# One hybrid encoder kernel, side work moved from a timed queue to a lower scheduling rank, and the hidden rows of layer 1 turned by quarters

## The chip, the core and the metric

The kernel runs on one core of a Trainium2 chip. The metric is the device time of one execution in microseconds (us); the median of three runs of the kernel before is 1550.26 us (1547.73 to 1551.45).

A core has a matrix engine (TensorE, PE in the profile; its weight loads are PEld), a vector engine (VectorE, DVE), a scalar engine (ScalarE, ACT), a general engine (GpSimd, POOL) and SyncE (SP), which here only issues DMA transfers. Each engine works off its own list of instructions in order and waits on semaphores for the others. Matrix products go to PSUM, eight banks of 128 x 512 words.

## The reference

x is 512 tokens by 2048. Two layers, each:

```python
h = rmsnorm(x, pre_norm_g[l])
z = h @ w_in[l]                       # 2048 x 5952: latents, conv inputs, memory query, gate
q_lat, kv_lat, k_pe, gb, gc, xin, q_mem, gate = split_cols(z)
a_out = mla_attention(q, k, v)        # 8 heads; q, k, v from the normalised latents, rotary part
c_out = short_gated_conv(gb, gc, xin, conv_w[l])
mem_n = rmsnorm(mem, mem_norm_g[l])   # 256 memory tokens
m_out = memory_attention(q_mem, mem_n, w_mk[l], w_mv[l])   # 4 heads
y = concatenate([a_out, c_out, m_out]) * silu(gate)        # 512 x 2048
x = x + rmsnorm(y @ w_o[l], post_norm_g[l])
```

All of it is float32.

## The kernel before

**Float32 products.** An operand is kept as a high part (a cast to fp32r, `wh` for weights) and a low part (operand minus high part, `wl`). A product is three matmuls, high*high, low*high, high*low: the helper `mm3`, L228 to L230. One *unit* is a weight piece of 128 x 1024 words: SP loads it into a raw buffer `wr` (L132), ACT makes `wh` (L157), DVE makes `wl` (L158), TensorE uses it in 12 matmuls of 512 columns. There are three buffers each for `wh` and `wl`, so the split of unit k waits until TensorE is through with unit k-3.

**Fewer products.** The two big projections (h @ w_in and y @ w_o) are made block-wise with seven products P1 to P7 in place of eight, as Winograd's form of Strassen's scheme has it. The price is side sums: sums `T` of weight blocks (DVE, L407, tiles of a pool `tf` with three buffers), and sums `S` of blocks of the activations, made in place (L373 to L385) and then split like the weights, high part on ACT (L233), low part on DVE (L234). `A` are the unsummed activation blocks, split in the same way. A *group* is two column blocks of the projection; its products come in *passes* (lists `HEAD`, `STEADY`, `SECOND`, `LATE`), and each result in PSUM is added by DVE to its slab (L445; `gb`, `gc`, `og` are such slabs).

**Layer edges.** Rows of x are normalised to `hs` (factor r from an ACT square sum, L561; product L567 in layer 0, on ACT L564 in layer 1, where the tile is called `og`), turned by TensorE against the identity into PSUM banks `hps` (L578, 16 transposes for a tile of 128 tokens), and taken to `hT` times the gain: on DVE for tiles 0 and 1 (L580), on ACT for tiles 2 and 3 (L584). The gains' columns `cols` come from a small transpose (L267, L269). Between the layers there are 16 *memory steps*: eight of keys (`mk`, four banks, 24 matmuls of 256 columns) and eight of values (`mv`, two banks, 12 of 512), whose weight pieces carry the gain (L162, L163). In them the tail of layer 0 (post-norm, residual: L1126 square, L1131 gain, L1164 sum, L1171 residual `xr`) runs and tiles 0 and 1 are turned, each as a whole; tiles 2 and 3 are turned in passes P1 and P2 of layer 1's projection.

**What sets the order.** PE and SP run in the order of the program's list of steps (`manual_schedule`); SP's loads run ahead of the steps by a count. DVE, ACT and POOL are put in order by a scheduler by each instruction's rank, which is normally the place where the program emits it. Side work does not stand in the list: `defer(cost, fn)` puts it into a queue; each step adds its `room` to a sum `spare` (at most 2.5), and the head of the queue is emitted when `spare` covers its cost; `until` empties the queue as far as a product needs it, `settle` wholly. In the queue stand the sums S1 to S4 (cost 2.4 each), the splits A11 and A22, the tables for the rotary part, the post-norm pieces (`scale`, 0.7) and the residual.

The residual's rows `xr` are loaded by SP (L1141) and the post-norm gain `g` too (L244), in the same list as the weights.

## Time and profile before

| | |
|---|---|
| median of three runs | 1550.26 us |
| the profiled execution | 1552.12 us |
| its span, first to last instruction | 1550.4 us |
| granted TensorE clock, mean | 0.994 |
| PE busy | 1500.4 us, 97% |
| DVE busy | 1289.0 us, 83% |
| ACT busy | 855.8 us, 55% |
| POOL busy | 41.6 us, 3% |
| DMA read and written | 259.59 MB, 14.68 MB |

1.7 us of the profiled execution lie outside its span. A row of the timeline gives start, duration, engine, line and operation, and in brackets how long the engine stood idle before it and on whom it waited; equal rows that follow each other are merged ("x3"), with their durations summed. A row overlaps the next one a little, so the pitch of an engine is read from the starts. "A:B" rows of the stage view give, for a stretch in us, the busy time of PE, PEld, DVE, ACT and POOL with their instruction counts, then the granted clock, the DMA share and GB/s.

### The profile page before, as it was taken

The page shows a single profiled execution, that of the slowest core. Times are in us where ns is not written, and L with a number is a line of the kernel's source. Part 1 is how long each engine was busy: PE and PEld are TensorE (multiplying, and loading weights), DVE is VectorE, ACT ScalarE, POOL GpSimd, SP SyncE. Part 2 cuts the span into 40 slices and gives each one's busy share as a digit, 9 for nine tenths or more (in the row PEclk, how much of TensorE's full clock was granted, in tenths as well). Part 3 has the DMA queues.
Part 4 walks back from the last instruction along what each step waited for, and adds up shares of the span by engine and source line. Part 5 has one row for each costly group of instructions (what it writes and reads, how often), then busy time and mean ns, then how long its engine had stood idle before and what let it go on. Part 6 is the DMA issues. An engine that isn't in the chain of part 4 may idle for free.

```text
span 1550.4 us, 20284 instructions
## 1 busy us (share of the span) xinstructions
PE 1500.4 (97%) x7613; PEld 1280.3 (83%) x7613; DVE 1289.0 (83%) x1646; ACT 855.8 (55%) x1315; POOL 41.6 (3%) x73
## 2 busy tenths in 40 slices
PE   8999999999999999998989999999999999999987
PEld 6778888998898888877778778888988888888866
DVE  5999889787977668899884999989788686689997
ACT  6633443455557768644586633443454587775543
POOL 1000000010000000000120000000010000000001
PEclk9999999999999999999999999999999999999999
DMA  6677656677482111566966677566666511037673
GB/s 254 195 220 236 196 178 180 178 217 237 150 267 83 42 42 57 174 213 211 349 207 227 205 221 229 187 191 177 184 211 207 164 42 42 28 96 224 210 241 140
DMA packets 147446, 275.59 MB, mean 178 GB/s; under 512 B 17340, under 2 KB 40212, under 8 KB 144020
## 3 DMA queue, kind: packets, MB, share of 16 engines
q1 hardware_dynamic: 144336, 257.48, 53.0%
q0 software_dynamic: 2880, 16.78, 2.9%
q8 instruction: 59, 0.97, 0.3%
q14 instruction: 39, 0.32, 0.1%
q10 hardware_dynamic: 132, 0.05, 0.0%
HBM read 259.59 MB, written 14.68 MB: 177 GB/s over the span
## 4 chain that ended last, share of the span: by engine, by line
PE 73%; DVE 16%; DMA 4%; issue 3%; ACT 3%; POOL 1%; SPq 0%; DVEq 0%; POOLq 0%; ACTq 0%
PE P L229 16%; PE P L230 16%; PE P L228 16%; DVE wl L158 5%; DVE T L407 4%; DMA wr<-in_w_o_dram 2%; PE ptp L989 2%; PE tps L747 1%; PE sc L228 1%; PE sc L229 1%; PE sc L230 1%; PE o L228 1%; PE o L229 1%; PE o L230 1%; PE sc L969 1%
## 5 line engine op out<-in xcount | busy, mean ns | idle before, releaser
L157 ACT CAST wh<-T 128x1024 fp32r<-128x1024 f32 (+1 forms) x220 | 226.1, 1029 | 309.8 <-PE P L230 209.1
L230 PE MATMUL P<-wh,S 128*128 128x512 f32 (+1 forms) x896 | 345.8, 386 | 10.6 <-DVE S L234 10.6
L229 PE MATMUL P<-wl,S 128*128 128x512 f32 (+1 forms) x896 | 346.6, 387 | 9.1 <-DVE wl L158 9.1
L228 PE MATMUL P<-wh,S 128*128 128x512 f32 (+1 forms) x896 | 347.5, 388 | 3.4 <-DVE og L445 3.4
L158 DVE TENSOR_TENSOR wl<-T,wh 128x1024 fp32r<-128x1024 f32 (+1 forms) x220 | 261.1, 1190 | 50.2 <-ACT wh L157 49.5
L157 ACT CAST wh<-wr 128x1024 fp32r<-128x1024 f32 (+1 forms) x188 | 194.7, 1042 | 183.9 <-PE P L230 138.1
L158 DVE TENSOR_TENSOR wl<-wr,wh 128x1024 fp32r<-128x1024 f32 (+1 forms) x188 | 223.7, 1195 | 70.4 <-ACT wh L157 69.4
L228 PE MATMUL P<-wh,A 128*128 128x512 f32 (+1 forms) x656 | 254.0, 387 | 2.0 <-ACT A L233 1.8
L229 PE MATMUL P<-wl,A 128*128 128x512 f32 (+1 forms) x656 | 252.5, 385 | 2.8 <-DVE wl L158 2.8
L230 PE MATMUL P<-wh,A 128*128 128x512 f32 (+1 forms) x656 | 252.1, 384 | 0.0
L229 PEld LDWEIGHTS P<-wl,S 128*128 128x128 f32 x896 | 169.0, 189 | 43.7 <-DVE wl L158 14.2
L230 PEld LDWEIGHTS P<-wh,S 128*128 128x128 f32 x896 | 168.8, 188 | 43.3 <-DVE S L234 13.1
L228 PEld LDWEIGHTS P<-wh,S 128*128 128x128 f32 x896 | 169.0, 189 | 34.1 <-ACT wh L157 4.3
L407 DVE TENSOR_TENSOR T<-wr,wr 128x1024 f32<-128x1024 f32 (+1 forms) x112 | 132.4, 1191 | 18.9 <-DMA wr<-in_w_in_dram 14.4
L229 PEld LDWEIGHTS P<-wl,A 128*128 128x128 f32 x656 | 123.6, 188 | 25.7 <-DVE wl L158 3.7
L228 PEld LDWEIGHTS P<-wh,A 128*128 128x128 f32 x656 | 123.5, 188 | 24.8 <-ACT A L233 2.0
L230 PEld LDWEIGHTS P<-wh,A 128*128 128x128 f32 x656 | 123.4, 188 | 22.9 <-DVE A L234 0.8
L407 DVE TENSOR_TENSOR T<-wr,T 128x1024 f32<-128x1024 f32 (+1 forms) x112 | 132.9, 1191 | 3.3 <-DMA wr<-in_w_o_dram 1.7
L975 ACT ACTIVATE P<-sc,nm 128x512 f32<-128x512 f32 (+1 forms) x96 | 60.4, 631 | 36.3 <-DVE nm L972 36.3
L972 DVE TENSOR_REDUCE nm<-sc 128x1 f32<-128x512 f32 (+1 forms) x96 | 56.9, 595 | 10.7 <-PE sc L970 8.6
L978 ACT ACTIVATE P<-P,rec 128x512 f32<-128x512 f32 (+1 forms) x96 | 62.6, 667 | 5.6 <-DVE rec L977 5.6
L234 DVE TENSOR_TENSOR PT<-ptp,PT 128x512 fp32r<-128x512 f32 (+1 forms) x96 | 56.4, 594 | 8.0 <-ACT PT L233 7.7
(257 smaller groups left out, 2263.1 us busy)
## 6 DMA issues: line engine op xcount, KB each, us to landing
wr<-in_w_in_dram SPq DMA_DIRECT2D x240, 512.0 KB, 4.6
wr<-in_w_o_dram SPq DMA_DIRECT2D x112, 512.0 KB, 4.9
wr<-in_w_in_dram SPq DMA_DIRECT2D x56, 416.0 KB, 3.9
wr<-in_w_mk_dram SPq DMA_DIRECT2D x16, 512.0 KB, 4.4
wr<-in_w_mv_dram SPq DMA_DIRECT2D x16, 512.0 KB, 4.1
wr<-in_w_uq_dram SPq DMA_DIRECT2D x24, 256.0 KB, 3.7
x<-in_x_dram SPq DMA_DIRECT2D x4, 1024.0 KB, 7.2
wr<-in_w_ukv_dram SPq DMA_DIRECT2D x8, 512.0 KB, 3.9
```

Source lines behind the costliest of these rows:

```text
L157: nc.scalar.copy(hi[:, :n], src)
L158: nc.vector.tensor_tensor(lo[:, :n], src, hi[:, :n].bitcast(F32), op=ALU.subtract)
L228: nc.tensor.matmul(ps, ah, bh, start=first, stop=False, **kw)
L229: nc.tensor.matmul(ps, ah, bl, start=False, stop=False, **kw)
L230: nc.tensor.matmul(ps, al, bh, start=False, stop=last, **kw)
L234: nc.vector.tensor_tensor(lo, src, hi.bitcast(F32), op=ALU.subtract)
L407: nc.vector.tensor_tensor(t, a, b, op=ALU.subtract)
L747: nc.tensor.transpose(ps[:, t * P:(t + 1) * P], view(t)[:, j * P:(j + 1) * P], G["ident"])
L972: nc.vector.tensor_reduce(nmax, ps, axis=AX.X, op=ALU.max, negate=True)
L975: nc.scalar.activation(pt, ps, AF.Exp, bias=nmax, accum_out=tot)
L978: nc.scalar.activation(pt, pt, AF.Copy, scale=rec)
L989: nc.tensor.transpose(ps[:, k * P:(k + 1) * P], pt[:, k * P:(k + 1) * P], G["ident"])
```

## The change

1. The queue is gone. `later(k, fn)` emits at once, with a rank that is k places later; sums S and split A22 get `SUMS` = 96, post-norm pieces `SOON` = 48, rotary tables `SLOW` = 200. Split A11 and the residual are emitted in place.
2. Raw buffers go from five to six, `tf` buffers from three to two; the square sum of the post-norm writes to a tile of its own (`junk`) and not to a `tf` buffer.
3. The 16 loads of `g2` (eight, 256 KB) and `xr` (eight, 1 MB) go from SP's queue to GpSimd's.
4. The start of layer 0 is written out by hand for DVE, ACT and POOL as well: `cols` right after the first `hs`, halves of tiles 0 and 1 in another order (the first half of tile 1 taken by ACT), and P1 begins after 24 transposes where there were 32.
5. In layer 1 all four tiles are turned among the memory steps, by quarters (four transposes, one bank): one after each of the 16 steps. The sums of the left operand are emitted after quarters 11 and 15.

```diff
-RAW, TF, PIECES, SLABS = 5, 3, 4, 19
+RAW, TF, PIECES, SLABS = 6, 2, 4, 19
+SOON, SUMS, SLOW = 48, 96, 200
...
-    def add(self, fn, units=(), room=0.0, ahead=None):
+    def add(self, fn, units=(), ahead=None):
...
-    def defer(self, cost, fn):
-        self.queue.append((cost, fn))
...
+    def later(self, k, fn):
+
+        at = self.tc.cur_priority
+        self.tc.cur_priority = at + k
+        fn()
+        self.tc.cur_priority = at + 1
...
-            spare = min(spare + room, 2.5)
-            while self.queue and spare >= self.queue[0][0]:
-                cost, put_off = self.queue.pop(0)
-                spare -= cost
-                put_off()
...
         for f in (one, two, four, three):
-            pr.defer(2.4, f)
+            pr.later(SUMS, f)
...
-    def transpose_rows(l, t, src, halves=(0, 1)):
+    def transpose_rows(l, t, src, quarters=range(4), on=None):
...
-            if t < 2:
+            if (on or (nc.vector if t < 2 else nc.scalar)) is nc.vector:
...
-        pr.defer(1.2, lambda: left.split("A22", tt, b[:, 8:, :]))
+        pr.later(SUMS, lambda: left.split("A22", tt, b[:, 8:, :]))
...
-                    row(st["g", g, j], post_norm_g[l, (2 * g + j) * 512:(2 * g + j + 1) * 512])
+                    nc.gpsimd.dma_start(st["g", g, j], post_norm_g[l, (2 * g + j) * 512:(2 * g + j + 1) * 512]
+                                        .partition_broadcast(P))
...
-                    junk = tf_p.tile([P, 1024], F32, tag="tf", name=nm("junk"))
-                    nc.scalar.activation(junk[:, :512], o, AF.Square, accum_out=st["ssq"][t][:, k:k + 1])
+                    nc.scalar.activation(G["junk"], o, AF.Square, accum_out=st["ssq"][t][:, k:k + 1])
...
-                pr.defer(0.7, scale)
+                pr.later(SOON, scale)
...
-                nc.sync.dma_start(st["x"][t], G["src"][t * P:(t + 1) * P, :])
+                nc.gpsimd.dma_start(st["x"][t], G["src"][t * P:(t + 1) * P, :])
...
-            for h in range(2):
-                for t in range(2):
-                    add(lambda t=t, h=h: transpose_rows(0, t, G[f"hs{t}"], (h,)))
-                    add(lambda t=t, h=h: left_half(t, (h,)))
-            add(lambda: first_rows(2))
-            add(lambda: first_rows(3))
+            def turn_half(t, h, on=None):
+                return lambda: transpose_rows(0, t, G[f"hs{t}"], (2 * h, 2 * h + 1), on)
+            add(turn_half(0, 0))
+            add(lambda: first_rows(1, (0,)))
+            add(pr.begin_prep(1))
+            add(lambda: left_half(0, (0,)))
+            add(pr.begin_prep(2))
+            add(turn_half(1, 0, nc.scalar))
+            add(lambda: first_rows(1, (1,)))
+            add(lambda: left_half(1, (0,)))
+            add(pr.begin_prep(3))
+            add(lambda: first_factor(2))
+            add(turn_half(0, 1))
         else:
             ms = mem_steps(l)
-            put(ms[:3])
+            put(ms[:1])
             add(use)
-            for t in range(2):
-                add(lambda t=t: pr.until(lambda: f"hs{t}" in G))
-                add(turn[t])
-                add(lambda t=t: left_half(t))
-                put(ms[3 + 4 * t:7 + 4 * t])
-            put(ms[11:])
+            for n in range(16):
+                t, q = n // 4, n % 4
+                add(lambda t=t, q=q: transpose_rows(l, t, G[f"hs{t}"], (q,)))
+                if t < 2 and q % 2:
+                    add(lambda t=t, q=q: left_half(t, (q // 2,)))
+                if t >= 2 and q == 3:
+                    add(lambda t=t: right_half(t - 2))
+                put(ms[n + 1:n + 2])
...
-                pr.defer(1.2, lambda: left.split("A11", p, a[:, :, :256]))
-                pr.defer(1.2, lambda: left.split("A22", p, b[:, :, 256:]))
+                left.split("A11", p, a[:, :, :256])
+                pr.later(SUMS, lambda: left.split("A22", p, b[:, :, 256:]))
```

How this moves instructions is seen in three places. The rows below are the engines' own lists, in order (line, operation, output<-inputs, shape; line numbers are those of the kernel in question, the numbers behind names only tell tiles apart).

**DVE, output projection of layer 0, first passes of its first group, before.** `wl` are the low parts of units, `T` weight sums, `y` and `S` the sums of the activations and their splits, `og<-og,P` results added to their slab.

```order
L445 TENSOR_TENSOR og_5797<-og_5797,P_704_6084 128x512
L234 TENSOR_TENSOR S_709_6168<-y_3439,S_709_6168 128x1024
L158 TENSOR_TENSOR wl_6176<-T_710_6173,wh_6175 128x1024
L158 TENSOR_TENSOR wl_6200<-T_713_6197,wh_6199 128x1024
L407 TENSOR_TENSOR T_716_6219<-wr_6143,T_713_6197 128x1024
L377 TENSOR_TENSOR y_3439<-y_3439,y_3752 128x4x256
L407 TENSOR_TENSOR T_719_6241<-wr_6171,T_716_6219 128x1024
L158 TENSOR_TENSOR wl_6222<-T_716_6219,wh_6221 128x1024
L407 TENSOR_TENSOR T_720_6263<-wr_6193,wr_6195 128x1024
```

**The same place now.** `wl_6200`, `wl_6224` and `wl_6246` here are the splits that are `wl_6176`, `wl_6200` and `wl_6222` above.

```order
L156 TENSOR_TENSOR wl_6200<-T_715_6197,wh_6199 128x1024
L371 TENSOR_TENSOR y_3447<-y_3447 128x4x256
L156 TENSOR_TENSOR wl_6224<-T_718_6221,wh_6223 128x1024
L227 TENSOR_TENSOR S_706_6092<-y_3447,S_706_6092 128x1024
L227 TENSOR_TENSOR S_707_6096<-y_3447,S_707_6096 128x1024
L435 TENSOR_TENSOR og_5806<-og_5806,P_711_6113 128x512
L435 TENSOR_TENSOR og_5817<-og_5817,P_712_6114 128x512
L227 TENSOR_TENSOR S_708_6100<-y_3805,S_708_6100 128x1024
L397 TENSOR_TENSOR T_721_6243<-wr_6167,T_718_6221 128x1024
L1120 TENSOR_TENSOR og_5806<-og_5806,g_709_6103 128x512
L1120 TENSOR_TENSOR og_5817<-og_5817,g_709_6103 128x512
L156 TENSOR_TENSOR wl_6246<-T_721_6243,wh_6245 128x1024
```

Between the second and the third of these splits there stood three whole-width operations (two weight sums and one sum of the activations); now there stand four (three splits `S` and one weight sum) and four of half width (two results and two post-norm products), and one sum of the activations stands ahead of the second.

**DVE, output projection of layer 0, pass P3/P1 of its second group, before.** `T_744` and `T_749` are the weight sums T3 and T1 of a chunk; `og<-og,g` is the post-norm's product.

```order
L1131 TENSOR_TENSOR og_5786<-og_5786,g_702_6075 128x512
L1131 TENSOR_TENSOR og_5797<-og_5797,g_702_6075 128x512
L445 TENSOR_TENSOR og_5788<-og_5788,P_732_6461 128x512 x2
L445 TENSOR_TENSOR og_5799<-og_5799,P_733_6462 128x512 x2
L1131 TENSOR_TENSOR og_5788<-og_5788,g_702_6075 128x512
L1131 TENSOR_TENSOR og_5788<-og_5788,g_701_6073 128x512
L1131 TENSOR_TENSOR og_5799<-og_5799,g_702_6075 128x512
L1131 TENSOR_TENSOR og_5799<-og_5799,g_701_6073 128x512
L158 TENSOR_TENSOR wl_6661<-wr_6585,wh_6660 128x1024
L158 TENSOR_TENSOR wl_6667<-wr_6615,wh_6666 128x1024
L407 TENSOR_TENSOR T_744_6617<-wr_6585,wr_6639 128x1024
L407 TENSOR_TENSOR T_749_6641<-wr_6639,wr_6615 128x1024
```

**The same place now** (`T_741` and `T_744`).

```order
L156 TENSOR_TENSOR wl_6552<-T_738_6549,wh_6551 128x1024
L397 TENSOR_TENSOR T_741_6626<-wr_6589,wr_6642 128x1024
L397 TENSOR_TENSOR T_744_6644<-wr_6642,wr_6624 128x1024
L156 TENSOR_TENSOR wl_6568<-wr_6509,wh_6567 128x1024
L435 TENSOR_TENSOR og_5806<-og_5808,P_732_6455 128x512
L435 TENSOR_TENSOR og_5817<-og_5819,P_733_6456 128x512
L156 TENSOR_TENSOR wl_6592<-wr_6529,wh_6591 128x1024
L435 TENSOR_TENSOR og_5808<-og_5808,P_735_6477 128x512 x2
L435 TENSOR_TENSOR og_5819<-og_5819,P_736_6478 128x512 x2
L1120 TENSOR_TENSOR og_5806<-og_5806,g_710_6105 128x512
L1120 TENSOR_TENSOR og_5817<-og_5817,g_710_6105 128x512
L156 TENSOR_TENSOR wl_6661<-wr_6589,wh_6660 128x1024
```

The two sums of the second chunk stood behind ten `og` operations and two splits; they now stand ahead of all of these.

**ACT, memory steps of layer 1, before.** `wh<-wr,cols` are the memory steps' weights (the last is step 16), `wh<-wr` without `cols` the first units of the projection, `Km` and `Vm` the results of keys and values.

```order
L162 ACTIVATE wh_7590<-wr_7516,cols 128x512 x2
L162 ACTIVATE wh_7622<-wr_7536,cols 128x512 x2
L157 CAST wh_7642<-wr_7568 128x1024
L233 CAST Km_7670<-mk_7188 128x256
L233 CAST Km_7670<-mk_7189 128x256
L233 CAST Km_7670<-mk_7190 128x256
L157 CAST wh_7681<-wr_7588 128x1024
L233 CAST Km_7670<-mk_7191 128x256
```

**The same place now.** `hT_7668<-hps_7669` takes the first quarter of tile 3 (quarter 12 of the 16, counted from 0), `hps_7698` the second, `hps_7746` the third.

```order
L226 CAST A_812_7617<-hT_7508 128x1024
L160 ACTIVATE wh_7680<-wr_7547,cols 128x512 x2
L155 CAST wh_7709<-wr_7588 128x1024
L226 CAST S_813_7621<-hT_7508 128x1024
L155 CAST wh_7757<-wr_7636 128x1024
L226 CAST S_814_7625<-hT_7508 128x1024
L226 CAST S_815_7629<-hT_7238 128x1024
L226 CAST S_816_7633<-hT_7508 128x1024
L570 ACTIVATE hT_7668<-hps_7669,cols 128x128 x4
L570 ACTIVATE hT_7668<-hps_7698,cols 128x128 x4
L226 CAST Km_7737<-mk_7208 128x256
```

The first two quarters of tile 3 now stand behind two casts of the projection's weights and four splits `S`; before, tiles 2 and 3 were taken further down, among the projection's units.

More of the change, by code (lines that the diff above doesn't have):

```diff
@@ L165, in prep @@
                 outs[c] = (hi[:, :n], lo[:, :n])
+        self.prep = prep
         c = 0
-        spare = 0.0
-        for units, fn, room, ahead in self.steps:
+        for units, fn, ahead in self.steps:
             n = len(units)
@@ L574, in transpose_rows @@
         g = G[f"g1_{l}"].rearrange("p (k o) -> p k o", o=1)
-        for q in [2 * h + i for h in halves for i in range(2)]:
+        for q in quarters:
             ps = bank("hps")
```

125 lines of the change are left out of this document (66 added, 59 removed).

## The prediction

> **What bounds the kernel now.** I first read the page's busy time, then for whom TensorE waits, and then the stages in which it does.
>
> ```profile
> PE 1500.4 (97%) x7613; PEld 1280.3 (83%) x7613; DVE 1289.0 (83%) x1646; ACT 855.8 (55%) x1315; POOL 41.6 (3%) x73
> ...
> PE P L229 <- DVE wl L158: 11.8, 14, 1.7
> PE P L230 <- DVE S L234: 10.6, 6, 2.9
> PE P L228 <- DVE og L445: 3.4, 2, 2.4
> PE hps L578 <- DVE hT L580: 3.2, 2, 2.8
> ```
>
> TensorE is busy for 97% of the span and the change takes no matmul away, so only its waits can be won. The waits' columns are us in total, times, longest. Nearly all are short waits for DVE: 22 of them, 25.8 us, for low parts, side sums and PSUM results. Over the whole program DVE has room (83%); it hasn't in some stages:
>
> ```profile
> 680.00:720.00 40.00, 38.70 (x171) 31.74 (x170) 38.63 (x43) 19.66 (x30) 0.00 (x0) 1.00 0.55 172
> 720.00:760.00 40.00, 35.33 (x154) 28.40 (x153) 32.59 (x31) 18.15 (x24) 1.61 (x3) 1.00 0.89 316
> 810.00:868.00 58.00, 57.95 (x317) 49.88 (x315) 37.51 (x44) 37.34 (x70) 1.14 (x2) 1.00 0.64 202
> 868.00:960.00 92.00, 86.50 (x369) 69.91 (x369) 87.26 (x85) 39.92 (x40) 0.00 (x0) 0.98 0.70 221
> ```
>
> The third number of a row is DVE: 38.63 of 40 us before 720, 87.26 of 92 in layer 1's projection, but 37.51 of 58 just ahead of that. So the order of DVE's work decides: what is moved from 868:960 into 810:868 is free, what is moved into a full stretch is paid in full. A wait costs more than itself where the granted clock falls behind it:
>
> ```profile
> 18.90:22.30 3.40, 3.36 (x7) 2.26 (x8) 3.40 (x6) 1.57 (x2) 0.00 (x0) 0.50 1.01 381
> 733.00:736.40 3.40, 2.80 (x11) 2.12 (x12) 3.40 (x5) 1.77 (x5) 0.00 (x0) 1.00 0.93 293
> 923.40:926.80 3.40, 3.40 (x10) 2.68 (x9) 3.29 (x4) 0.86 (x1) 0.00 (x0) 0.51 0.55 155
> ```
>
> Shortly after the waits at 18.89 and 921.96 (below) the clock was 0.50 for 3.4 us, which does the work of 1.7 us; after the one at 733.03 it stayed 1.00. I charge 1.5 us for such a stretch.
>
> The pitch of the work, from starts:
>
> ```profile
> 711.78 1.31 DVE L1131 TENSOR_TENSOR og<-og,g 128x512 f32<-128x512 f32 x2
> 713.00 2.36 DVE L158 TENSOR_TENSOR wl<-wr,wh 128x1024 fp32r<-128x1024 f32 x2
> 715.27 2.36 DVE L407 TENSOR_TENSOR T<-wr,wr 128x1024 f32<-128x1024 f32 x2
> ...
> 716.90 0.39 PE L228 MATMUL P<-wh,A 128*128 128x512 f32 x1
> 719.62 0.39 PE L228 MATMUL P<-wh,S 128*128 128x512 f32 x1
> ```
>
> A full-width DVE operation takes 1.135 us (713.00 to 715.27 for two), one of half width 0.61, and the 12 matmuls of a unit 2.72 (716.90 to 719.62). A split is one operation, with a weight sum two, 2.27: DVE gains 0.45 us a unit there, and each operation more between two splits costs 1.135 of its lead, which three low-part buffers limit.
>
> **Start (a gain of 4.4 us).**
>
> ```profile
> 12.71 3.49 DVE L158 TENSOR_TENSOR wl<-wr,wh 128x1024 fp32r<-128x1024 f32 x3
> 16.12 0.24 DVE L269 COPY cols<-cps 128x88 f32<-128x88 f32 x1
> ...
> 16.41 0.66 PE L578 MATMUL hps<-ident,hs 128*128 128x128 f32 x4 [1.82 <-DVE cols L269]
> 18.89 0.80 PE L228 MATMUL P<-wh,A 128*128 128x512 f32 x1 [1.81 <-ACT A L233]
> ...
> PE P L230 <- DVE S L234: 3.8, 2, 2.6
> PE P L229 <- DVE wl L158: 2.3, 3, 0.9
> ```
>
> `cols` stands behind three splits, 3.4 us (12.71 to 16.12), and the last transposes wait for it. Now it stands ahead of them, and eight transposes (0.87) are no longer ahead of P1. P1 starts 3.4 to 4.3 us earlier; I take 4.1. The last two rows are the waits of the first 160 us: 3.8 and 2.3 us, to which a half-clock stretch belongs; all of it, 7.6 us, goes, as the sums are now emitted elsewhere. In their place come two bursts: in the new order four operations stand between the splits of the 11th and 12th units (with the split 5.7 us for a unit of 2.72, 3.0 late), and further on two `S`, two results of half width and two sums ahead of a split (6.9 for 2.72, 4.2 late). 4.1 + 7.6 - 7.2 = 4.5; I take 4.4. Bounds: the bursts swallowed by DVE's lead, 8; a half-clock stretch behind each and half of the old waits left, -2.
>
> **Output projection, first passes (a loss of 6.5).** Before, from `wl_6176` to `wl_6222` there are five full-width operations, 5.7 us for two units (5.4). Now, from `wl_6200` to `wl_6246`, there are seven and four of half width: 7 x 1.135 + 4 x 0.61 = 10.4. That is 4.7 more, twice (both layers have it), 9.4. The waits that stood a little later there,
>
> ```profile
> 672.09 0.50 PE L230 MATMUL P<-wh,S 128*128 128x512 f32 x1 [1.17 <-DVE S L234]
> ...
> PE P L230 <- DVE S L234: 1.5, 1, 1.5
> ```
>
> (layer 0; the second row is the same place of layer 1) were for an `S` that is now made earlier, so 1.2 + 1.5 go: -9.4 + 2.7 = -6.7; I take 6.5. Bounds: 0 with DVE three units ahead, as the late split then finds its unit still covered by 8 us of matmuls; 10 if nothing goes.
>
> **Output projection, late passes (a gain of 10).** In layer 0 between 700 and 745, and in layer 1 from 1430 on:
>
> ```profile
> PE P L229 <- DVE wl L158: 3.6, 3, 1.7
> PE P L228 <- DVE og L445: 2.4, 1, 2.4
> ...
> PE P L229 <- DVE wl L158: 4.0, 4, 1.7
> PE P L228 <- DVE og L445: 1.0, 1, 1.0
> ...
> 722.66 1.05 ACT L157 CAST wh<-wr 128x1024 fp32r<-128x1024 f32 x1 [4.50 <-DMA wr<-in_w_o_dram]
> 720.68 2.36 DVE L407 TENSOR_TENSOR T<-wr,wr 128x1024 f32<-128x1024 f32 x2 [0.78 <-DMA wr<-in_w_o_dram]
> ...
> 731.60 8.37 SPq L1141 DMA_DIRECT2D xr<-in_x_dram  x2
> ```
>
> 11.0 us in all. Their root is raw weights that land late: ACT waits 4.50 us and DVE 0.78 for them, because a chunk holds three of five buffers until its sums are made, and these stood behind ten `og` operations. Now they stand ahead of the `og` operations, there is a sixth buffer, and SP's list holds no `xr` whose wait stops the weights behind it (two issues took 8.37 us at 731.60). I take 10 of the 11; bounds 4 (only the DMA waits go, 5.3 us in layer 0, and not all reaches TensorE) and 11.
>
> **Memory steps of layer 1 (a loss of 2.7).**
>
> ```profile
> 792.09 1.25 PE L578 MATMUL hps<-ident,og 128*128 128x128 f32 x8 [2.83 <-DVE hT L580]
> ...
> 845.54 4.25 ACT L584 ACTIVATE hT<-hps,cols 128x128 f32<-128x128 f32 x16
> 849.55 1.17 ACT L157 CAST wh<-wr 128x1024 fp32r<-128x1024 f32 x1
> 850.49 1.18 ACT L233 CAST A<-hT 128x1024 fp32r<-128x1024 f32 x1
> ```
>
> A tile turned whole waits for its banks' evacuation: six of eight banks are keys and values, so 2.83 at 792.09, and 3.2 with the second. By quarters a bank has two steps to come free (2.72 us for one of values, by the pitch above); the 3.2 go. But quarter 14 needs the bank of quarter 12, and ACT evacuates that behind the cast of the projection's second unit, which waits until TensorE is through with step 15, the step just ahead of quarter 14. So TensorE waits for that cast and three `S` splits (0.95 each, 849.55 to 850.49) and a quarter's evacuation (a fourth of 845.54 to 849.55, 1.0): 4.8, with semaphores and DVE's sum for the last `S` 5. Behind it on ACT stand `Km` and the units' casts. A second place: half of a step's weights behind two evacuations and an `A` on DVE (2 x 0.61 + 1.135 = 2.4), of which I take 0.9. 3.2 - 5.0 - 0.9 = -2.7. Bounds: +3.2, and -7 with both in full and ACT late.
>
> **Projection of layer 1 (a gain of 5).** Waits between 865 and 960:
>
> ```profile
> PE P L230 <- DVE S L234: 4.1, 2, 2.9
> PE P L229 <- DVE wl L158: 1.4, 2, 0.9
> 921.96 0.50 PE L230 MATMUL P<-wh,S 128*128 128x512 f32 x1 [2.90 <-DVE S L234]
> ```
>
> 5.5 us and a half-clock stretch, 7.0. All eight sums are now made before this stretch, in the one with 20 us of room. The first units' casts and splits stand behind quarter 14's backlog; I let them take back 2 of it, +5. Bounds 1 and 7.
>
> **The rest.** The heads, with two `tf` buffers: rotated queries of the next tile must wait for the turn of this one, and TensorE makes that turn ahead of the scores that need ACT next; nothing, +-2. The loads on GpSimd's list: what stands behind them there is the reload of the memory operands, whose own wait ends later than SP's for `xr` did (739.97),
>
> ```profile
> 752.59 0.55 POOL L687 DMA_DIRECT2D mH<-mTd  x1 [295.99 <-DVE wl L158]
> ```
>
> (after 296 us without work), so nothing; if the reload waited, the first memory step would be late by as much. Half-clock stretches behind the new waits of 4.2, twice 4.7, and 5.0 us: the trace has two behind three, I charge two of four, -2.9.
>
> By the Trainium skill, "TensorE: Matmul & The Clock Gate", section "Part 1: The HAM clock gate (the 'warmup' mystery)", the clock halves only after an idle window of about 3.4 us; here it halved after 1.81 and 2.90, so the trace does not bear that out as a bound from below. By it all four new waits would cost a stretch each, 3.1 us more than in my sum.
>
> **Sum**: 4.4 - 6.5 + 10 - 2.7 + 5 - 2.9 = +7.3. The profiled execution took 1552.1 us with 1550.4 of span; it becomes 1544.8. The median of the runs lies 1.9 below it, so I forecast **1543.0**, own range 1536 to 1549.
>
> **Rivals.**
> *The lead swallows the new waits.* A sixth raw buffer and earlier sums could leave DVE three units ahead when the bursts come. Then 6.5, 5.0 and 2.9 of the losses don't come: 1543 - 14.4 = 1528.6; with half of it 1536. For it: 20 us of room just ahead of the projection, and no DMA wait that eats the lead any more. Against it: 38.63 of 40 us at the first passes.
> *No change.* The gains of the late passes and of layer 1's projection are only half, 7.5 less, as DVE's total work there is the same and its waits merely move: 1550.5. For it speaks that the change takes no DVE work away.
> *Slower: two sum buffers.* A sum T may not be written until the split two sums back is done, and that one waits for a low-part buffer; DVE has one sum (1.19 with its row, 1.135 by pitch) less lead wherever TensorE waits for it. Place: the passes with a weight sum for every unit, in both projections. Price: 22 waits x 1.135 = 25 us if each is longer by one, 12.5 if half are: 1543 + 12.5 = 1555.5. It decides from 11 of the 22 on. Against it: DVE's own order already puts a sum one ahead at most in most rows.
>
> **Chances.** Forecast 0.45, swallowed 0.25, no change 0.15, slower 0.15. A measurement tells 0.3%, 4.7 us, from no change, so faster is below 1545.6: two thirds of the forecast's range, the whole second case: 0.56. Within: a third of the first, most of the third, some of the last: 0.28. Slower: 0.16. The range reaches half-way into the last case and to the second case's full price: 1529 to 1555.
>
> **What would show it.** P1 starts near 14.8 in the changed profile; waits of 4 to 5 us for `wl` near 655 and 1417; waits for `wl` and `og` below 1 us from 700 to 745; one wait of `hps` for ACT's `hT` of about 5 us near 825 and none of 2.8 for DVE's; DVE below 90% and no wait for `S` in layer 1's projection. Wrong it would be if DVE's order left TensorE the same sum of waits in other places, about 37 us, or if waits for a weight sum grew all over.

## The result, and the profile after

| | before | changed |
|---|---|---|
| median of runs (range, number), us | 1550.86 (1547.73 to 1552.01, 4) | 1569.27 (1565.95 to 1572.20, 4) |
| ratio, 95% interval | | 1.0121 [1.0092, 1.0151] |
| profiled execution, its span, us | 1552.12, 1550.4 | 1566.91, 1565.1 |
| mean granted clock | 0.994 | 0.991 |

The changed kernel is slower by 1.2%. I had forecast 1543.0 us and a range up to 1555. The page of the changed kernel gives the engines' busy times (us, share of the span, instructions):

```profile
PE 1503.3 (96%) x7613; PEld 1281.2 (82%) x7613; DVE 1298.9 (83%) x1642; ACT 858.9 (55%) x1323; POOL 47.7 (3%) x89
```

TensorE's waits in it (us in total, times, longest):

```profile
PE P L222 <- DVE wl L156: 15.4, 18, 2.3
PE P L221 <- ACT wh L155: 10.5, 6, 3.1
PE hps L564 <- ACT hT L570: 7.4, 1, 7.4
PE P L221 <- DVE og L435: 4.2, 2, 2.2
PE mv L222 <- DVE wl L161: 2.4, 1, 2.4
...
PE P L223 <- DVE S L227: 0.8, 1, 0.8
```

The work is the same. The waits for side sums `S` are nearly gone (10.6 us before, 0.8 now). In their place stand waits for the high parts `wh`, one wait of 7.4 us for a quarter of turned rows, and longer waits for `wl`. All of TensorE's waits sum to 51.4 us, where they summed to 39.6 before.

Waits alone miss what a lower clock costs, so I used a second measure that holds both. All kernels here run the same 7613 TensorE instructions. Each kind has a pitch, the median from one start to the next (0.227 us for a matmul of 512 columns, 0.187 for 416, 0.120 for 256, 0.109 for a transpose of 128); the pitches sum to 1476.4 us in every one of them. The **time lost** up to an instruction is its start less the pitches of all that are ahead of it. The table cuts the program at the same TensorE instructions in every kernel and gives the us lost in each stage; the letters stand for runs that are told of further on.

| stage (its time in the kernel before) | before | changed | e3 | e2 | e5 | e8 | e9 | e10 | e11 | b1 | b2 |
|---|---|---|---|---|---|---|---|---|---|---|---|
| start, to 74 | 13.6 | 8.5 | 12.2 | 9.8 | 12.7 | 13.3 | 12.7 | 12.3 | 9.7 | 14.7 | 14.9 |
| layer 0, projection, to 120 | 6.2 | 7.0 | 2.8 | 7.9 | 2.8 | 2.8 | 2.8 | 2.8 | 7.9 | 4.8 | 5.9 |
| the rest of it, to 493 | 3.3 | 9.9 | 2.8 | 11.5 | 3.0 | 2.8 | 3.3 | 2.9 | 11.3 | 11.3 | 3.3 |
| heads, to 627 | 4.2 | 2.3 | 3.5 | 2.3 | 3.6 | 4.7 | 4.7 | 4.7 | 2.2 | 1.5 | 2.6 |
| output projection, first passes, to 721 | 3.5 | 9.5 | 7.6 | 8.8 | 7.7 | 4.2 | 3.8 | 1.2 | 8.7 | 6.7 | 8.1 |
| its late passes, to 787 | 5.6 | 5.6 | 7.4 | 5.3 | 10.8 | 10.9 | 2.3 | 2.3 | 1.6 | 1.9 | 5.2 |
| last pass, first memory steps, to 833 | 5.9 | 5.6 | 8.2 | 5.5 | 4.6 | 4.6 | 3.9 | 5.4 | 3.9 | 6.0 | 5.4 |
| memory steps to the last, to 862 | 0.1 | 9.5 | 9.7 | 0.1 | 0.1 | 0.1 | 0.1 | 0.1 | 9.0 | 0.1 | 0.0 |
| layer 1, projection, to 951 | 8.1 | 2.1 | -0.1 | 3.8 | 0.7 | 0.7 | 0.7 | 0.7 | 2.0 | 8.4 | 8.0 |
| the rest of it and heads, to 1406 | 5.5 | 9.1 | 7.9 | 9.8 | 7.3 | 9.0 | 8.9 | 7.3 | 9.1 | 8.3 | 7.8 |
| output projection, first passes, to 1438 | 1.8 | 6.0 | 6.6 | 6.5 | 6.3 | 1.5 | 0.0 | 0.0 | 6.4 | 3.2 | 0.9 |
| its late passes, to 1538 | 6.4 | 3.8 | 5.6 | 3.6 | 5.6 | 5.6 | 1.9 | 2.9 | 1.5 | 6.2 | 6.4 |
| sum | 64.1 | 78.9 | 74.3 | 74.7 | 65.1 | 60.2 | 45.1 | 42.5 | 73.3 | 73.1 | 68.4 |

From 64.1 to 78.9 is 14.8 us, and the spans differ by 14.7. So the table holds the loss: +6.6 in the steady part of layer 0's projection, +6.0 and +4.2 in the first passes of the two output projections, +9.4 in the last memory steps, +3.6 in the rest of layer 1. Against it stand -6.0 in layer 1's projection, -5.1 at the start, -2.6 in the last late passes and -1.9 in the heads.

How far a cell can be trusted is seen up to layer 0's heads: there the changed kernel, e2 and e11 run the same instructions in the same order, and their cells still differ by up to 1.6 us, the four rows together by 3.8 (27.7 to 31.5). So the smallest of these differences are not clear of chance; b2, which is the kernel before but for its loads, has 2.6 in the heads and 7.8 in the rest of layer 1 (before: 4.2 and 5.5).

The stages of the changed kernel that answer to those shown of before (busy us of PE, PE's weight loads, DVE, ACT, POOL; granted clock, DMA share, GB/s):

```profile
720.00:760.00 40.00, 36.90 (x160) 30.06 (x161) 35.29 (x35) 18.24 (x24) 3.18 (x6) 1.00 0.84 299
826.00:868.00 42.00, 34.57 (x184) 29.71 (x183) 33.47 (x36) 28.81 (x54) 1.14 (x2) 0.92 0.58 182
868.00:960.00 92.00, 90.39 (x398) 74.31 (x397) 78.74 (x77) 37.54 (x38) 0.00 (x0) 1.00 0.70 219
668.20:671.60 3.40, 3.40 (x9) 2.63 (x10) 3.34 (x4) 2.10 (x2) 0.00 (x0) 0.50 0.52 154
847.70:851.10 3.40, 3.40 (x11) 2.83 (x11) 1.50 (x5) 2.82 (x11) 0.58 (x1) 0.50 0.00 0
```

DVE did get room in layer 1's projection: 78.74 of 92 us, where it had 87.26. The memory steps pay for it: TensorE is busy for 34.57 of 42 us at a clock of 0.92. The last two rows lie in half-clock stretches behind the two kinds of new waits. Each of these lasts 6.8 us in all: from 666.9 to 673.7, and from 844.4 to 851.2, of which 3.0 us fall into the wait itself.

### The profile page after: what moved, and what is told of

It reads as the page before. It is cut to its first block, busy times and chain, and to the rows that moved or that the text cites. A ratio compares the mean times of both kernels' runs of the same rounds, so it can differ in the third digit from the quotient of the medians.

```text
span 1565.1 us, 20352 instructions
## 1 busy us (share of the span) xinstructions
PE 1503.3 (96%) x7613; PEld 1281.2 (82%) x7613; DVE 1298.9 (83%) x1642; ACT 858.9 (55%) x1323; POOL 47.7 (3%) x89
## 4 chain that ended last, share of the span: by engine, by line
PE 48%; issue 24%; DVE 17%; ACT 6%; DMA 4%; POOL 1%; DVEq 0%; SPq 0%; POOLq 0%; ACTq 0%
PE P L222 10%; PE P L223 10%; PE P L221 10%; DVE wl L156 4%; DMA wr<-in_w_o_dram 4%; DVE T L397 3%; PE ptp L979 1%; DVE og L435 1%; PE tps L737 1%; DVE S L227 1%; DVE xr L1160 1%; ACT wh L155 1%; ACT P L965 1%; DVE og L1120 1%; PE qps L223 1%
## 5 line engine op out<-in xcount | busy, mean ns | idle before, releaser
L221 PEld LDWEIGHTS P<-wh,S 128*128 128x128 f32 x896 | 169.1, 189 | 45.1 <-ACT wh L155 15.5
L222 PEld LDWEIGHTS P<-wl,A 128*128 128x128 f32 x656 | 123.4, 188 | 33.5 <-DVE wl L156 12.2
L965 ACT ACTIVATE P<-sc,nm 128x512 f32<-128x512 f32 (+1 forms) x96 | 60.2, 627 | 37.6 <-DVE nm L962 37.5
```

Of the source, the lines that this page charges most:

```text
L221: nc.tensor.matmul(ps, ah, bh, start=first, stop=False, **kw)
L222: nc.tensor.matmul(ps, ah, bl, start=False, stop=False, **kw)
L965: nc.scalar.activation(pt, ps, AF.Exp, bias=nmax, accum_out=tot)
```

## The experiments

My theory after the result: four parts lose, each in its own place: the third sum buffer given up for a sixth raw one, the crowded side sums, the right half's sums ahead of the last quarters, and the post-norm's products that come too early. The rival: all of it is one loss, the two sum buffers (or the loads on GpSimd), and the waits elsewhere follow from it. Times of an experiment stand beside runs of the kernel before on the same chip. Where two versions are compared through their medians, this is said; the chips can differ by 2 us in it, as the kernel before had medians from 1549.96 to 1552.02.

### One part at a time

**e3: the buffers back to five raw and three sums.**

```diff
-RAW, TF, PIECES, SLABS = 6, 2, 4, 19
+RAW, TF, PIECES, SLABS = 5, 3, 4, 19
```

> The changed kernel with five raw and three sum buffers, as before the change. Theory B (with two sum buffers DVE has one sum less lead wherever TensorE waits for it): 10 to 15 us faster, 1553 to 1559 us, and waits for splits of weight sums shorter all over. Theory A: within 3 us of the changed kernel; in the late passes of the output projections the waits for raw weights grow by 1 to 4 us a layer.

1561.54 us (1559.79 to 1562.95, 4 runs), 1.0069 [1.0054, 1.0084]; 7.7 us under the changed kernel's median. In the table the gain stands where a sum buffer should matter: 9.9 to 2.8 in the steady part of layer 0's projection and 7.0 to 2.8 just ahead of it. The wait for the quarter stays the same:

```profile
PE hps L564 <- ACT hT L570: 7.4, 1, 7.4
```

**b1: the kernel before with six raw and two sum buffers.** As in the change, the squares' scratch, which before lay in a sum buffer, got a tile of its own, and the identity and the set-up rows went from tiles of their own to shared small ones.

```diff
-RAW, TF, PIECES, SLABS = 5, 3, 4, 19
+RAW, TF, PIECES, SLABS = 6, 2, 4, 19
...
-                    junk = tf_p.tile([P, 1024], F32, tag="tf", name=nm("junk"))
-                    nc.scalar.activation(junk[:, :512], o, AF.Square, accum_out=st["ssq"][t][:, k:k + 1])
+                    nc.scalar.activation(G["junk"], o, AF.Square, accum_out=st["ssq"][t][:, k:k + 1])
```

> The kernel before with the pools of the change alone: six raw and two sum buffers, a tile of its own for the square sum, the constants' tiles made smaller for it. The queue, the loads on SP, the start and the whole-tile turns stay. Theory B (the third sum buffer is DVE's lead over TensorE): 6 to 12 us slower than the kernel before, 1556 to 1562 us, with the new waits for splits in the passes between 100 and 350 us and at the output projections' begin. Theory A (only the clumped order costs): within 3 us of the kernel before.

1561.23 us (4 runs) against 1552.02 (17): 1.0058 [1.0043, 1.0073], 9.2 us. In the other order, with the old queue, the exchange costs about the same. The place shows how. First DVE of the kernel before, then of b1, at the same results of layer 0's projection (start, duration, out<-in):

```profile
125.86 1.22 DVE L407 TENSOR_TENSOR T<-wr,T 128x1024 f32<-128x1024 f32 x1
127.36 1.23 DVE L158 TENSOR_TENSOR wl<-T,wh 128x1024 fp32r<-128x1024 f32 x1 [0.28 <-ACT wh L157]
...
134.44 0.68 DVE L445 TENSOR_TENSOR gc<-gc,P 128x512 f32<-128x512 f32 x1
135.04 1.22 DVE L158 TENSOR_TENSOR wl<-T,wh 128x1024 fp32r<-128x1024 f32 x1
```

```profile
127.02 1.23 DVE L158 TENSOR_TENSOR wl<-T,wh 128x1024 fp32r<-128x1024 f32 x1 [0.28 <-ACT wh L157]
...
134.10 0.68 DVE L445 TENSOR_TENSOR gc<-gc,P 128x512 f32<-128x512 f32 x1
134.69 1.22 DVE L407 TENSOR_TENSOR T<-wr,T 128x1024 f32<-128x1024 f32 x1
135.83 0.69 DVE L631 TENSOR_TENSOR gc<-gc,xi 128x512 f32<-128x512 f32 x1
136.43 1.22 DVE L407 TENSOR_TENSOR T<-wr,wr 128x1024 f32<-128x1024 f32 x1
137.57 2.50 DVE L158 TENSOR_TENSOR wl<-T,wh 128x1024 fp32r<-128x1024 f32 x2
```

With three buffers the sum that the split at 135.04 reads is made at 125.86, ahead of nine operations of half width on the results and of two splits that have sums of their own. With two, a buffer for it comes free only when the split at 127.02 has read the sum there. By then the results are due, the sum stands behind them (134.69), and its split comes at 137.57, 2.5 us later. TensorE waits there:

```profile
137.12 0.49 PE L228 MATMUL P<-wh,A 128*128 128x512 f32 x1 [0.39 <-ACT wh L157]
138.84 0.50 PE L229 MATMUL P<-wl,A 128*128 128x512 f32 x1 [1.22 <-DVE wl L158]
```

b1 also shows what the exchange is good for: in layer 0's late passes it loses 1.9 us instead of 5.6. Both runs move a raw and a sum buffer at once; the rows above tie the loss to the sums at this place. A kernel with six raw and three sum buffers was not run.

**e2: the right half's side sums behind the 16th quarter.**

```diff
-                if t >= 2 and q == 3:
-                    add(lambda t=t: right_half(t - 2))
                 put(ms[n + 1:n + 2])
+            for tt in range(2):
+                add(lambda tt=tt: right_half(tt))
```

> The changed kernel with one edit: the sums of both pairs of layer 1's hidden rows are emitted after the sixteenth quarter, and not after quarters 11 and 15. Theory A: TensorE's wait of 7.4 us for ACT's evacuation of quarter 12 (near 847 us) goes with its half-clock stretch, 9 us; the sums now fall into the projection's first two passes, where they may cost up to 3 us; 1560 to 1563 us. Theory B and C: the wait stays or its time appears elsewhere, no change in sum.

1563.14 us (4 runs), 1.0082 [1.0067, 1.0097]; 6.1 under the changed kernel's median. The stage of the last memory steps goes from 9.5 to 0.1, and 1.7 of it come back in the projection behind it (2.1 to 3.8). In the changed kernel TensorE waits, and ACT's timeline tells for what:

```profile
847.42 1.12 PE L564 MATMUL hps<-identr,og 128*128 128x128 f32 x4 [7.43 <-ACT hT L570]
...
842.07 1.04 ACT L226 CAST S<-hT 128x1024 fp32r<-128x1024 f32 x1 [1.06 <-DVE hT L367]
844.34 1.99 ACT L226 CAST S<-hT 128x1024 fp32r<-128x1024 f32 x2 [1.23 <-DVE hT L371]
846.24 2.16 ACT L570 ACTIVATE hT<-hps,cols 128x128 f32<-128x128 f32 x8
```

The evacuations that free quarter 14's bank start at 846.24, behind the casts of `S`. Two of these waited another 1.06 and 1.23 us for DVE's sums, which are made in place in `hT`.

**e1: the four sums apart.** Ranks of 96, 96, 288 and 480 instead of 96 for all four.

```diff
-        for f in (one, two, four, three):
-            pr.later(SUMS, f)
+        for k, f in ((1, one), (1, two), (3, four), (5, three)):
+            pr.later(k * SUMS, f)
```

> The changed kernel with one edit: the four side sums of a pair no longer share one lower rank (96 places), they are put apart: S1 and S2 at 96, S4 at 288, S3 at 480. Theory A (sums of one rank stand together in DVE's order, and TensorE waits for the split behind them): the stretch in which the output projection's first passes lose 7 us against the kernel before in layer 0 (near 667 us) and 8 us in layer 1 (near 1440 us), half-clock stretches included, shrinks to 2 us or less each, the 5 us lost near 78 us mostly go too; the whole is 10 to 17 us faster than the changed kernel, 1552 to 1559 us. Theory B (two sum buffers) and theory C (loads through GpSimd): no change, 1565 to 1572 us.

1571.96 us (4 runs), 1.0137 [1.0122, 1.0152]: no gain. Layer 0's first passes lose 8.9 instead of 9.5. With two sum buffers, moving the side sums doesn't help there.

**e4: the 16 loads back on SP's list.**

```diff
-                    nc.gpsimd.dma_start(st["g", g, j], post_norm_g[l, (2 * g + j) * 512:(2 * g + j + 1) * 512]
-                                        .partition_broadcast(P))
+                    row(st["g", g, j], post_norm_g[l, (2 * g + j) * 512:(2 * g + j + 1) * 512])
...
-                nc.gpsimd.dma_start(st["x"][t], G["src"][t * P:(t + 1) * P, :])
+                nc.sync.dma_start(st["x"][t], G["src"][t * P:(t + 1) * P, :])
```

> The changed kernel with the 16 loads of residual rows and post-norm gains back on SP's queue. Theory C (loads through GpSimd cost time): several us faster. Theory A: within 2 us of the changed kernel; if SP's wait for a residual slab stops the weights behind it, as in the kernel before, up to 3 us slower in the late passes of the output projections.

1577.33 us (1572.76 to 1585.37, 4 runs), 1.0182 [1.0144, 1.0220]: 8 us above the changed kernel's median. 7.5 us of the profiled execution's loss stand in the last stage (3.8 to 11.3), and there most of it is one wait, for the last weight sum's high part:

```profile
1550.73 0.79 PE L221 MATMUL P<-T4h,A 128*128 128x512 f32 x1 [4.74 <-ACT T4h L155]
```

In that kernel all four casts of `T4h` stand on ACT behind the squares of a result that DVE takes only after four residual operations. Why the scheduler's order comes out so with the loads back on SP stays open.

**b2: the kernel before, with the 16 loads on GpSimd.** The same lines the other way, in the old order.

> The kernel before with one part of the change: the 16 loads of post-norm gains and residual rows on GpSimd's list. If SP's wait for the residual's slabs holds up the weights of the late passes, as the prediction had it, the waits near 733 and 741 us and the same of layer 1 shrink: 2 to 5 us faster. If those weights were issued ahead of it anyway and DVE's work sets these waits: within 2 us of the kernel before.

1556.93 us (10 runs) against 1551.19 (24): 1.0039 [1.0023, 1.0054], 5 to 6 us. The loss is in layer 0's first passes (3.5 to 8.1). DVE's timeline there, in the kernel before:

```profile
637.59 1.29 DVE L234 TENSOR_TENSOR PT<-ptp,PT 128x512 fp32r<-128x512 f32 x2
...
640.19 1.23 DVE L407 TENSOR_TENSOR T<-wr,T 128x1024 f32<-128x1024 f32 x1 [0.17 <-DMA wr<-in_w_o_dram]
```

And in b2, with GpSimd's first gains and TensorE's wait:

```profile
633.80 1.23 DVE L407 TENSOR_TENSOR T<-wr,T 128x1024 f32<-128x1024 f32 x1 [1.54 <-DMA wr<-in_w_o_dram]
638.25 1.22 DVE L407 TENSOR_TENSOR T<-wr,T 128x1024 f32<-128x1024 f32 x1 [1.97 <-DMA wr<-in_w_o_dram]
...
639.99 1.28 DVE L234 TENSOR_TENSOR PT<-ptp,PT 128x512 fp32r<-128x512 f32 x2
...
634.37 1.10 POOL L1105 DMA_DIRECT2D g<-in_post_norm_g_dram  x2 [176.78 <-PE ptp L989]
...
641.33 0.39 PE L229 MATMUL o<-PT,V 128*128 128x256 f32 x1 [3.13 <-DVE PT L234]
```

The weights of these two sums come earlier in b2, where SP has no gains to issue ahead of them: they land at 633.70 and 638.15, in the kernel before at 640.09 and 642.04. But both sums now stand ahead of the last head's `PT` in DVE's list, DVE stops there for weights, and TensorE waits 3.13 us for `PT` (0.24 before). The gains' transfers can't have made the first of DVE's waits: it was over at 633.80, and GpSimd issued its first gain at 634.37. They may have lengthened the second, as its weight took 6.5 us to land beside them, the first 3.8. So by these rows what costs is DVE's order; why it changes with the loads' place stays open, as in e4.

### Parts together

**e5: e3 and e2 together.**

> The changed kernel with five raw and three sum buffers and the side sums of layer 1 behind the sixteenth quarter. If the two causes are separate places, their gains of 8 and 6 us add: 1553 to 1558 us. If they are the same time counted twice (the lead lost at one place is lost at the next anyway): 1559 to 1562 us.

1554.30 us (10 runs), 1.0013 [1.0003, 1.0024]. Through medians 15.0 us under the changed kernel, and the two parts alone gave 7.7 + 6.1 = 13.8: two losses that add up, so not one. The largest losses left against before, by the table, are the two first passes (7.7 and 6.3) and layer 0's late passes (10.8); the changed kernel, with its sixth raw buffer, loses 5.6 in the last.

**e6: e5 with the sums apart (e1's edit).**

> The one before (three sum buffers, sums behind the sixteenth quarter) with the side sums S put apart in rank (96, 96, 288, 480) as well. With two sum buffers putting them apart gained nothing. If that was because DVE then had no weight sums made ahead, it gains now: the 5 us lost near 663 us and the same place of layer 1 shrink to 2 us or less, 6 to 10 us in all, 1544 to 1551 us. If rank is not what makes these waits: within 3 us of the one before.

1558.25 us (7 runs), 1.0040 [1.0028, 1.0051]. The first passes do gain now, 7.7 to 4.3 and 6.3 to 1.5. But the beginning of layer 0's projection (second row of the table, 2.8 in e5) loses 15.6 (3.7 of it are taken from the row ahead, so 9 in all), as the same function makes the hidden rows' sums there. ACT of e6:

```profile
82.78 1.04 ACT L226 CAST S<-hT 128x1024 fp32r<-128x1024 f32 x1 [6.83 <-DVE hT L375]
83.73 1.07 ACT L443 COPY gb<-P 128x512 f32<-128x512 f32 x2
```

A cast of `S` waits 6.83 us for a sum whose rank is now far down DVE's list, and behind it on ACT stands the copy that frees a result's bank. TensorE's `P` at 84.36 waits 11.71 us for it.

**e7: e6 with the residual at a lower rank still.** The last post-norm piece of a tile emits the residual, which so had rank 48 already; now it has 48 more.

```diff
-                        residual(l, st, t)
+                        pr.later(SOON, lambda: residual(l, st, t))
```

> The one before with the residual, which the change emits in place, at the post-norm's lower rank (48 places) as well. If the 2.5 us wait near 781 us, for a split that stands behind two residual operations which wait for GpSimd's factor, is made by the residual's rank: that wait goes, 2 to 3 us faster in layer 0, and nothing in the tail. Otherwise no change.

1557.07 us (5 runs), 1.0034 [1.0021, 1.0047]. The wait near 781 does go: e6 waits 2.35 us for a split at 783.9 and 2.44 for a step's weights at 808.4, e7 at neither place. The late passes go from 9.1 (e6) to 7.5, the stages behind hardly move, and the medians' 1.2 us lie within both ranges, so as times the two are not told apart.

**e8: e5 with the sums apart in the output projections alone.**

```diff
+        far = (1, 1, 1, 1) if left.by_tokens else (1, 1, 3, 5)
+        for k, f in zip(far, (one, two, four, three)):
+            pr.later(k * SUMS, f)
```

> The changed kernel with three sum and five raw buffers, layer 1's side sums behind the sixteenth quarter, and the side sums put apart in rank (96, 96, 288, 480) in the output projections alone. With them apart everywhere the output projections' first passes lost 5 us less in each layer, but TensorE waited 12 us near 84 us for an evacuation on ACT. So this should have the first without the second: 1543 to 1547 us, faster than the kernel before by 0.3 to 0.6%.

1551.07 us (12 runs) against 1551.19 (24): 1.0004 [0.9991, 1.0018]. It is level with the kernel before. The first passes lose 4.2 and 1.5 us instead of e5's 7.7 and 6.3; as whole times the two are hardly told apart, as the intervals of their ratios overlap. So the crowd does cost about what I priced it for, but spreading it pays only with a third sum buffer (e1 had two).

**e9: e8 with the post-norm's pieces at rank 144 instead of 48.** The number moves the squares, the products and, from the last of them, the residual.

```diff
-SOON, SUMS, SLOW = 48, 96, 200
+SOON, SUMS, SLOW = 144, 96, 200
```

> The one before with the post-norm pieces at rank 144 instead of 48. If the 4 us that are left in the late passes of each output projection come from post-norm products standing between sums and splits on a DVE without room, they move behind the pass and 2 to 4 us go in each layer: 1537 to 1542 us. If the pieces are then missed by the residual and the memory steps, as much comes back near 780 us: 1543 to 1548 us.

1537.44 us (7 runs), 0.9927 [0.9900, 0.9954]: 13.6 under e8's median. The late passes go from 10.9 to 2.3 and from 5.6 to 1.9.

**e11: the changed kernel with that one number alone.**

> The changed kernel with one edit: the post-norm pieces at rank 144 instead of 48. If the rank of the post-norm's products makes the late passes' waits by itself, the 3 to 4 us lost near 720 to 740 us and as much in layer 1 go: 6 to 10 us faster, 1559 to 1564 us. If it helps only once DVE has its third sum buffer and the side sums stand apart: under 3 us.

1560.17 us (5 runs) against 1550.66 (8): 1.0058 [1.0037, 1.0078], 9.1 under the changed kernel's median, with 5.6 to 1.6 and 3.8 to 1.5 in the late passes. (The two profiled executions lie only 5.7 us apart, so the late passes hold all of their difference.) DVE in layer 0's late passes, first the changed kernel, then e11:

```profile
718.12 1.29 DVE L1120 TENSOR_TENSOR og<-og,g 128x512 f32<-128x512 f32 x2
...
721.60 2.49 DVE L1120 TENSOR_TENSOR og<-og,g 128x512 f32<-128x512 f32 x4
...
735.53 1.23 DVE L397 TENSOR_TENSOR T<-wr,T 128x1024 f32<-128x1024 f32 x1 [1.23 <-DMA wr<-in_w_o_dram]
...
738.09 0.68 DVE L435 TENSOR_TENSOR og<-og,P 128x512 f32<-128x512 f32 x1
```

```profile
724.58 0.68 DVE L1120 TENSOR_TENSOR og<-og,g 128x512 f32<-128x512 f32 x1
725.18 1.22 DVE L156 TENSOR_TENSOR wl<-wr,wh 128x1024 fp32r<-128x1024 f32 x1
726.31 0.68 DVE L1120 TENSOR_TENSOR og<-og,g 128x512 f32<-128x512 f32 x1
...
732.59 1.28 DVE L1120 TENSOR_TENSOR og<-og,g 128x512 f32<-128x512 f32 x2
```

At rank 48 six products run in two lumps between 718 and 724, 3.8 us of work that no matmul asks for yet; splits, then weight loads, then sums move back behind them. At rank 144 they go into gaps behind splits, most of them singly.

**e10: e9 with the gains' loads back on SP's list** (the first hunk of e4's diff; the residual's loads stay on GpSimd).

> The kernel with the four edits (three sum buffers, sums behind the sixteenth quarter, apart in the output projections, post-norm pieces at rank 144) and the eight loads of the post-norm gains back on SP's list; the residual's loads stay on GpSimd's. In the old order GpSimd issued all four gains of a layer near 635 us, among the weights' loads, and DVE then waited 1.5 and 2.0 us for weights. If that is what the loads on GpSimd cost, the waits for PT near 637 us (2.2) and 1387 us (1.5) shrink to under 0.5: 2 to 4 us faster. If not: within 2 us.

1534.57 us (1531.65 to 1536.32, 4 runs) against 1550.66 (8): **0.9890 [0.9867, 0.9913]**, faster than both kernels. Against e9 this is 2.9 us by medians, and the intervals of the two ratios overlap; the wait that b2 pointed to does shrink, and DVE has both sums behind the last head's `PT` again (635.39 and 637.66, `PT` at 633.01). TensorE's waits for `PT` in e9, then in e10:

```profile
PE o L222 <- DVE PT L227: 4.0, 3, 1.9
```

```profile
PE o L222 <- DVE PT L227: 1.3, 3, 0.9
```

On e10's page TensorE is busy for 98% of the span.

## Why the prediction was wrong

My sum was a gain of 7.3 us; the profiled execution lost 14.7. The terms, in the prediction's order:

| term | predicted | lost or won (table) |
|---|---|---|
| start and its bursts | +4.4 | +4.3 |
| (steady projection of layer 0) | 0 | -6.6 |
| output projections, first passes | -6.5 | -10.2 |
| late passes | +10 | +2.6 |
| memory steps of layer 1, and the pass ahead | -2.7 | -9.1 |
| projection of layer 1 | +5 | +6.0 |
| heads; rest of layer 1 | 0 | +1.9; -3.6 |
| half-clock stretches | -2.9 | in the terms above (about -8.4) |

**Late passes (+10): the step that failed most.** I took the root to be raw weights that land late, and wanted the waits gone by earlier sums, a sixth buffer and `xr` off SP's list. The buffer did its part: in the old order b1 wins 3.7 us in layer 0 (0.2 in layer 1), and in the changed kernel ACT waits for no weight in these passes (5.0 and 5.6 us before). `xr` was no part of it: b2 takes it off SP's list and loses 5.2 and 6.4 us where the kernel before loses 5.6 and 6.4. What I put at nothing is what the queue had held until there was room and now runs at rank 48: the post-norm's products and the residual. TensorE's waits in layer 0's late passes were 4.7 us before. Now 2.5 are left near 739, where I had foretold less than 1, and 2.3 stand anew at 780.68, behind a residual that itself waited for GpSimd's `r`:

```profile
738.92 0.47 PE L221 MATMUL P<-wh,S 128*128 128x512 f32 x1 [1.94 <-DVE og L435]
...
775.81 2.48 DVE L1160 SCALAR_TENSOR_TENSOR xr<-og,r,xr 128x1024 f32<-128x1024 f32 x2 [1.50 <-POOL r L233]
779.40 2.35 DVE L156 TENSOR_TENSOR wl<-T,wh 128x1024 fp32r<-128x1024 f32 x2
...
780.68 0.50 PE L222 MATMUL P<-wl,A 128*128 128x512 f32 x1 [2.34 <-DVE wl L156]
```

So the stage wins nothing (5.6 to 5.6). e11 leaves the loads and the buffers alone and moves only the post-norm's pieces: the wait at 780.68 goes, 1.4 are left near 741, and the stage wins 4.0. How much of this is the products' and how much the residual's wasn't taken apart.

**Two sum buffers: a rival at 0.15 whose mechanism was true, at nothing in the sum.** The mechanism, the place (passes with a weight sum for each unit) and roughly the size held: 12.5 us was my price for half of the waits; b1 and e3 measured 9.2 and 7.7, net of what the sixth raw buffer wins. I held against it that DVE's order puts a sum one ahead at most "in most rows". The rows at 125.86 and 135.04 show the flaw: in a few places it stands two ahead, and these are the ones where a burst of results lies between the sum and its split. That takes the third buffer. In the sum itself I had charged it at nothing. Even with it charged, 1555.5, the forecast would have stayed 14 us short.

**Quarter 14: right place, too small.** One wait of `hps` for ACT's `hT` and none for DVE's, as foretold; 7.43 us instead of 5.0, and with the half clock behind it the stage lost 9.4 (9.5 less 0.1). It stood near 847, where I had 825. I had let the casts of `S` run back to back at 0.95 each, and put DVE's share into a rounding. They alternate with sums that DVE makes in the same tile; the waits of 1.06 and 1.23 us are nearly all of the 2.4 that I missed. The 3.2 us of waits for a whole tile's evacuation did go. New waits took them back: one of 1.4 at 810.13 for a step's high part, and one of 2.4 at 805.18 for a step's low part (the row `mv`). The last has the size and nearly the place of the second wait that I named (2.4, of which I had taken 0.9), but that is luck: I had two evacuations and an `A` ahead of the step's weights, and the rows have two residual operations, which waited for GpSimd again, and an `A`:

```profile
800.84 2.48 DVE L1160 SCALAR_TENSOR_TENSOR xr<-og,r,xr 128x1024 f32<-128x1024 f32 x2 [1.20 <-POOL r L233]
803.24 1.22 DVE L227 TENSOR_TENSOR A<-hT,A 128x1024 fp32r<-128x1024 f32 x1
804.38 1.41 DVE L161 SCALAR_TENSOR_TENSOR wl<-wr,cols,wh 128x512 fp32r<-128x512 f32 x2
```

**First passes: right cause, mis-sized.** 6.5 foretold, 10.2 measured. The waits themselves are shorter than I had them (3.7 and 3.9 us, for 4.7 each); the clock behind them took about 4.8 by an estimate from the half-clock stretches (below), which I had put in a term of its own. They show as waits for `wh` first, for `wl` after: the sum `T` that ACT casts stands behind the `S` splits too, so the high part is late before the low part is.

```profile
666.68 0.61 PE L221 MATMUL P<-wh,S 128*128 128x512 f32 x1 [3.09 <-ACT wh L155]
667.95 0.80 PE L222 MATMUL P<-wl,S 128*128 128x512 f32 x1 [0.65 <-DVE wl L156]
```

**Right:** the start (P1 at 14.17 us, where I had 14.8) with the bursts that take part of it back, and layer 1's projection: +6.0 for +5, DVE at 86% of it (78.74 of 92), no wait for `S`. In the start the size is luck in part: its two bursts show as waits of 1.9 and 3.3 us where I had 3.0 and 4.2, and a half-clock stretch makes up the rest.

**GpSimd's loads at nothing: wrong for the old order.** I weighed only what stands behind them on GpSimd. In b2 DVE's order changes with them, and that costs 5.7 us by the medians. In the changed order itself this wasn't measured alone (e4 mixes it with the wait at the end); there TensorE waits 0.45 us for the last head's `PT`.

**Half clock: mis-sized.** I charged two stretches for four new waits, 2.9 us. All four came: at a clock of 0.50 from 79.9 to 83.2 (behind waits of 2.50 and 0.76), from 666.9 to 673.7 (behind 3.09), up to 851.2 (behind 7.43) and from 1441.8 to 1445.2 (behind 3.10). By an estimate, half of the time in which TensorE could work in them, they cost 8.4 us. Behind 1.94 (738.92) and 2.34 (780.68) the clock stayed at 1.00. I had also misread the kernel before: it has four such stretches, not two (also from 111.0, behind 2.56 us, and from 496.7), and the wait of 1.81 at 18.89 that I named had another of 1.82 at 16.41 ahead of it, with 0.66 us of transposes between. A cleaner case is e9, where one wait of 1.93 us was enough:

```profile
636.97 0.38 PE L222 MATMUL o<-PT,V 128*128 128x256 f32 x1 [1.93 <-DVE PT L227]
637.20:640.60 3.40, 3.40 (x15) 3.11 (x15) 1.54 (x2) 0.36 (x1) 0.00 (x0) 0.51 1.01 377
```

The Trainium skill, "TensorE: Matmul & The Clock Gate", section "Part 1: The HAM clock gate (the 'warmup' mystery)", wants an idle window of about 3.4 us; here the clock halved behind this wait of 1.93 and behind 2.90 in the kernel before, so the window is no bound from below.

## What to carry to other kernels

A queue that holds side work until there is room sets two things, when it runs and how far apart; a fixed lower rank sets one number for each kind, and a kind (here the sums and the post-norm's pieces) needs its own, found from the stage where it lands. Before trading a buffer of one pool for another, look for the longest burst that stands between an operand's making and its use: the pool must hold what is needed at the end of the burst, not on the average. And when loads move to another engine's list, read the other engines' lists again: in b2 and e4 it was the order on DVE and ACT that changed and cost time.

## What the runs showed of the hardware that I had not expected

The granted clock depends on more than the length of the last wait: it halved behind 1.93 us in e9 and stayed at 1.00 behind 2.34 (780.68) in the changed kernel and 2.83 (792.09) in the kernel before. A half-clock stretch lasted 3.4 us in most places and 6.8 in two of the changed kernel.
